# First two row blocks turned unscaled by the identity, 1/rms applied when v is read out and to the turned blocks afterwards

## The chip, the cores and the metric

The kernel runs on one core of a Trainium2 chip. The metric is device time in microseconds for one execution. Before the change three runs gave 1469.04, 1468.01 and 1468.40 us, a median of 1468.4 us. One more execution was profiled: 1468.83 us, of which 1467.0 us lie between the first and the last instruction of the core.

The engines named below are PE (matrix multiplication; PEld is its weight load), ACT (activations and copies), DVE (element-wise work), POOL, and SP, which here only issues transfers (DMAs). Each engine works through its own instructions in the order in which the program left them.

## The reference

One step of a layer with a recurrent branch and an attention branch. The part that the change touches is its start: the rows are RMS-normalised, turned and multiplied by the columns of `w_in` for v (1024 of them) and for the forget logits (16).

```
def rms_norm(x, g):
    y = xf * lax.rsqrt(jnp.mean(xf * xf, axis=-1, keepdims=True) + EPS)
    return (y * g).astype(x.dtype)

xn = rms_norm(x, g_pre)
z = xn @ w_in
xa, ga, q, k, v, gb, fl, ma, mb = jnp.split(z, ...)
logf = jax.nn.log_sigmoid(fl + b_f)
```

`x` has 1024 prompt rows and 64 sample rows of 1024 channels. v and logf are outputs of their own, and all later projections read the same normalised rows.

## The kernel before

**Tiles.** Rows go in blocks of 128 (blocks 0 to 7 are the prompt, block 8 the sample). PE contracts over channels, so every block is turned: eight 128x128 pieces, one for each channel group k. A turned block is kept as a high and a low part, `xh` (ACT copies it from PSUM with rounding) and `xl` (DVE subtracts). Weights are split in the same way: for each k a load `wv_raw` of 128x1024 (`load_wv`, two of the eight go to halves of `w_raw`) is copied to `wvh` by ACT and gives `wvl` on DVE (`split_wv`). The 16 forget columns come by a load of their own, `wf_raw`, 128 x 8 x 16 values in runs of 64 bytes, and stand behind the v columns in `wvh` and `wvl`.

**v of blocks 0 and 1.** `rows(b, ks)` multiplies block b by the weights of the groups ks: three passes (high by high, low by high, high by low) into three PSUM accumulators of 346, 346 and 348 columns, the last with the forget columns. A block needs all eight k, so the accumulators of both blocks stay open while the weights land, and PE alternates between the blocks. `evac_v` copies a finished accumulator out (`v_sb`) and sends it to memory.

**Turning.** For blocks 0 and 1 the inverse rms comes first (`rstd_diag`: a square with a sum on ACT, some small DVE steps with one square root on ACT between them), is put on a diagonal `dg`, and `turn_diag` multiplies x by this diagonal, so the turned values arrive scaled. Only `g_pre`, as a column `gT` per channel group, is left for ACT and DVE to apply (`x_hi`, `x_lo`). Blocks 2 to 8 are normalised first (`norm_x`: square, inverse rms, `scale_x` on DVE into the one buffer `xn`) and turned by the identity (`turn_x`, tile `tp`).

**What sets the order.** PE's order is written by hand for the whole program. For the opening, down to `norm_x(2)`, ACT's and DVE's orders are by hand too (`opening`); SP's and the later ACT and DVE work is ordered by a scheduler when the program is built. Dependences on PSUM are kept per bank: ACT and DVE take turns in reading one bank.

**Start of the clock.** 36 multiplications of the identity (`wake`, L440) run on PE before data are there, with the turning of `g_pre` (`g_p`, L439) among them.

**After the opening.** A loop goes over blocks 2 to 8: three accumulators each, with the next blocks turned at given places (`turn_at`). In it block 3 is turned after the first third of block 2, block 4 after block 2, block 5 after the first third of block 3, and so on. Then come sums of the turned blocks (`ra`, `rb`, `rc`), the column panels (`panel_steps`, `quad`), attention and the output stages. PE's order there is by hand as well.

Of the kernel before, what the change touches and what calls it, by code (L numbers as in the profile page):

```python
# [7 lines left out]
F32 = mybir.dt.float32  # L8
# [58 lines left out]
def hybrid_step(tc, a, o):  # L67
# [11 lines left out]
    def f(ap):  # L79
        return ap.bitcast(F32)  # L80

    def copy_act(out, in_, scale=1.0):
        return act.activation(out=out, in_=in_, func=AF.Copy, scale=scale)  # L83
# [42 lines left out]
    def tiny(n, name, w=1, tag=None):  # L126
        return small.tile([P, w], F32, name=name, tag=tag or name)[:n, :]
# [65 lines left out]
    def run(steps):  # L193
        for _ in steps:
            pass
# [188 lines left out]

    turned = {}

    def rstd_diag(b):
        x, junk = x_in[b], p1x.tile([P, D], F32, name="xn", tag="xn", bufs=1)  # L390
        r = tiny(P, "r_r")
        if b == 0:
            c, c_ = slice(0, D // 2), slice(D // 2, D)
            ss, rest = tiny(P, "ss"), tiny(P, "ss_")
            act.activation(out=junk[:, c], in_=x[:, c], func=AF.Square, accum_out=ss)
            dve.tensor_tensor_reduce(out=junk[:, c_], in0=x[:, c_], in1=x[:, c_], scale=1.0 / D, scalar=EPS,
                                     op0=ALU.mult, op1=ALU.add, accum_out=rest)
            rstd_of(ss, r, 1.0 / D, rest=rest)
        else:
            ss = tiny(P, "ss")  # L400
            act.activation(out=junk[:, :], in_=x[:, :], func=AF.Square, accum_out=ss)
            yield
            rstd_of(ss, r, 1.0 / D)
        dg = p1x.tile([P, P], F32, name="dg", tag="dg", bufs=2)
        dve.tensor_scalar(out=dg[:, :], in0=ident[:, :], scalar1=r, scalar2=None, op0=ALU.mult)
        turned[b] = dg
        yield

    def turn_diag(b):
        x, dg = x_in[b], turned[b]  # L410
        turned[b] = [p1t.tile([P, 4, P], F32, name="tp", tag="tp") for _ in range(2)]
        for k in range(KT):
            pe.matmul(turned[b][k // 4][:, k % 4, :], x[:, k * P:(k + 1) * P], dg[:, :], start=True, stop=True)

    def x_hi(b, ks):
        for k in ks:
            copy_act(xs[k][0][:, b * P:(b + 1) * P], turned[b][k // 4][:, k % 4, :], scale=gT[:, k:k + 1])

    def x_lo(b, ks):
        for k in ks:  # L420
            h, l = (t[:, b * P:(b + 1) * P] for t in xs[k])
            dve.scalar_tensor_tensor(out=l, in0=turned[b][k // 4][:, k % 4, :], scalar=gT[:, k:k + 1], in1=f(h),
                                     op0=ALU.mult, op1=ALU.subtract)

    g8 = p1.tile([KT, P], F32, name="g8")
    gT = p1.tile([P, KT], F32, name="gT")
    load_x(0)
# [4 lines left out]
    load_wv(1)  # L432
    for k in range(2, KT):
        load_wv(k)
    wake = p1t.tile([P, 512], F32, name="wake", tag="tp")
    g_p = mm.tile([P, 512], F32, name="g_p", tag="acc")
    for i in range(WAKE):
        if i == WAKE - 8:
            pe.transpose(g_p[:, :KT], g8[:, :], ident[:KT, :KT])  # L439
        pe.transpose(wake[:, :P], ident[:, :], ident[:, :])  # L440

    def weights(k, c):
# [1 line left out]
        return wvh[:, k, c0:c0 + w], wvl[:, k, c0:c0 + w]  # L444


    pair = [[p1v.tile([P, 512], F32, name="vacc", tag="vacc") for _ in VCH]]
    pair.append([p1v.tile([P, 512], F32, name="vacc", tag="vacc"),
                 mm.tile([P, 512], F32, name="acc", tag="acc"), mm.tile([P, 512], F32, name="acc", tag="acc")])

    def rows(b, ks):
        for k in ks:
            xh, xl = (t[:, b * P:(b + 1) * P] for t in xs[k])
            for p in (0, 2, 1):
                for c, (_, w) in enumerate(VCH):
                    wh, wl = weights(k, c)
                    pe.matmul(pair[b][c][:, :w], xl if p == 2 else xh, wl if p == 1 else wh,  # L457
                              start=(k == 0 and p == 0), stop=(k == KT - 1 and p == 1))

    opening = tc.manual_schedule(engines={act.engine, dve.engine})  # L460
    opening.__enter__()
    run(rstd_diag(0))
    dve.tensor_copy(gT[:, :], g_p[:, :KT])
    turn_diag(0)
    second = rstd_diag(1)
    split_wv(0)
    next(second)
    x_hi(0, [0])
    x_lo(0, [0])
    copy_act(wvh[:, :, D:], wf_raw[:, :, :])  # L470
    sub(dve, wvl[:, :, D:], wf_raw[:, :, :], f(wvh[:, :, D:]))
    x_hi(0, [1])
    x_lo(0, [1])
    rows(0, [0])
    run(second)
    split_wv(1)
    rows(0, [1])
    turn_diag(1)
    for ks in (range(2, 4), range(4, KT)):
        x_hi(0, ks)  # L480
        x_lo(0, ks)
    x_hi(1, (0, 1))
    x_lo(1, (0, 1))
    split_wv(2)
    rows(1, (0, 1))
    x_hi(1, range(2, KT))
    x_lo(1, range(2, KT))
    sp.dma_start(g_pre[:, :], a["g_pre"].partition_broadcast(P))
    load_x(2)
# [13 lines left out]
    def evac_v(b, c, acc):  # L503
        _, n, t0 = x_src[b]
        v_out = o["v_prompt"][t0:t0 + n, :] if b < NBLK else o["v_sample"]
        c0, w = VCH[c]
        wv = min(w, D - c0)
        v_sb = p1.tile([P, VCH[-1][1]], F32, name="v_sb", tag="v_sb", bufs=3)
        copy_act(v_sb[:n, :wv], acc[:n, :wv])
        if b == NBLK:  # L510
            lo = p1.tile([DEC, VCH[-1][1]], F32, name="v_lo", tag="v_lo", bufs=1)
            copy_act(lo[:, :w], acc[DEC:, :w])
            dve.tensor_tensor(out=v_sb[:n, :wv], in0=acc[:n, :wv], in1=lo[:, :wv], op=ALU.add)
        act.dma_start(v_out[:, c0:c0 + wv], v_sb[:n, :wv])
        if wv < w:
            dve.tensor_tensor(out=fl[:n, b, :], in0=acc[:n, wv:w], in1=bf[:n, :], op=ALU.add)
            if b == NBLK:
                dve.tensor_tensor(out=fl[:n, b, :], in0=fl[:n, b, :], in1=lo[:, wv:w], op=ALU.add)

    for k in range(2, 6):  # L520
        split_wv(k + 1)
        rows(0, [k])
        rows(1, [k])
    split_wv(7)
    norm_x(2)
    opening.__exit__(None, None, None)
    rows(0, (6, 7))
    for c in range(3):
        evac_v(0, c, pair[0][c])
    rows(1, [6])  # L530
# [1 line left out]
    rows(1, [7])  # L532
    for c in range(3):
        evac_v(1, c, pair[1][c])

# [1602 lines left out]
```

## Time and profile before

| | |
|---|---|
| median of three runs | 1468.4 us (1468.01 to 1469.04) |
| profiled execution | 1468.83 us |
| its span on the core | 1467.0 us |
| granted PE clock, mean | 0.996 |
| DVE busy | 59% |
| ACT busy | 49% |
| v rows of block 0 finished on PE | 36.37 us |
| block 2 turned on PE | 37.80 us |
| first v rows of block 2 on PE | 40.10 us |

Times in the last three rows, and in every timeline row, are counted from the first instruction. A timeline row has start, duration, engine, source line, operation, output and inputs, shape and count, and in brackets the idle time of the engine before it with what ended it. A window row has the stretch, its length, busy time of engines with instruction counts, the granted PE clock, the busy share of the transfer engines, and GB/s. "x16" at L413 are eight multiplications of which each shows as two records.

### The profile page before, as it was taken

How to read it: one execution, taken by the hardware profiler on the slowest of the kernel's cores; microseconds unless marked ns; L12 is line 12 of the kernel's file. 1: busy time of each engine (PE TensorE's matmuls, PEld its weight loads, DVE VectorE, ACT ScalarE, POOL GpSimd, SP SyncE). 2: the span in 40 equal slices, each digit the busy share in tenths (PEclk: the TensorE clock that was granted, in tenths of full speed). 3: DMA queues.
4: the chain of work that ended last, by engine and by line, in shares of the span. 5: the costliest groups of instructions: out<-in, count | busy, mean ns of one | idle time of the engine just before them, and what ended most of it. 6: DMA issues, size and time to landing. Idle time of an engine off the chain costs nothing.

```text
span 1467.0 us, 26370 instructions
## 1 busy us (share of the span) xinstructions
PE 1442.0 (98%) x10117; PEld 1419.7 (97%) x10117; DVE 871.6 (59%) x1571; ACT 718.0 (49%) x1388; POOL 276.3 (19%) x363
## 2 busy tenths in 40 slices
PE   9999999999999999999999999999999999999997
PEld 8998999999999999999999999999999999999997
DVE  5564756665525666666556557798755454347644
ACT  4423444443215566656555557877543333334633
POOL 0012314323113333333223210000023000000001
PEclk9999999999999999999999999999999999999999
DMA  5367456655276565646556242121386534214111
GB/s 205 108 130 97 122 167 185 186 164 136 75 215 160 119 147 135 142 115 158 92 125 157 51 101 49 50 57 33 130 269 214 194 130 141 85 37 164 47 48 44
DMA packets 140793, 182.85 MB, mean 125 GB/s; under 512 B 22788, under 2 KB 111404, under 8 KB 140668
## 3 DMA queue, kind: packets, MB, share of 16 engines
q1 hardware_dynamic: 122684, 154.90, 40.3%
q10 hardware_dynamic: 17680, 25.64, 5.0%
q8 instruction: 80, 1.31, 0.4%
q0 software_dynamic: 304, 0.62, 0.1%
q14 instruction: 45, 0.37, 0.1%
HBM read 122.65 MB, written 58.46 MB: 123 GB/s over the span
## 4 chain that ended last, share of the span: by engine, by line
PE 91%; DVE 3%; ACT 3%; DMA 2%; issue 1%; ACTq 0%; SPq 0%; DVEq 0%
PE quad L786 17%; PE acc L163 16%; PE acc L164 16%; PE acc L165 16%; PE tp L1132 4%; PE pv L1160 3%; PE pv L1162 3%; PE s L1110 2%; PE s L1111 2%; PE vacc L163 1%; PE vacc L164 1%; PE vacc L165 1%; PE vacc L457 1%; DMA out_v_prompt<-v_sb 1%; DMA wv_raw<-in_w_in 1%; DMA q<-d_q 1%
## 5 line engine op out<-in xcount | busy, mean ns | idle before, releaser
L163 PE MATMUL acc<-xh,wh 128*128 128x364 f32 (+1 forms) x768 | 253.6, 330 | 3.1 <-ACT st L83 3.1
L164 PE MATMUL acc<-xl,wh 128*128 128x364 f32 (+1 forms) x768 | 252.5, 329 | 0.0
L165 PE MATMUL acc<-xh,wl 128*128 128x364 f32 (+1 forms) x768 | 252.4, 329 | 0.0
L163 PEld LDWEIGHTS acc<-xh,wh 128*128 128x128 f32 x768 | 145.2, 189 | 4.1 <-ACT st L83 3.4
L164 PEld LDWEIGHTS acc<-xl,wh 128*128 128x128 f32 x768 | 145.1, 189 | 0.5
L165 PEld LDWEIGHTS acc<-xh,wl 128*128 128x128 f32 x768 | 144.7, 188 | 0.0
L86 DVE TENSOR_TENSOR wl<-w_raw,wh 128x1024 fp32r<-128x1024 f32 (+1 forms) x66 | 76.9, 1168 | 64.1 <-ACT wh L83 56.2
L1090 DVE CUSTOM_DVE_ANT_0 s<-s,mask 128x1024 f32<-128x1024 f32 (+7 forms) x128 | 95.5, 767 | 26.1 <-PE s L1111 25.8
L83 ACT ACTIVATE wh<-w_raw 128x1024 fp32r<-128x1024 f32 (+1 forms) x66 | 64.3, 976 | 76.6 <-PE acc L164 35.1
L1095 POOL TENSOR_SCALAR pb<-pb,sm 128x896 f32<-128x896 f32 (+1 forms) x64 | 61.5, 961 | 203.8 <-DVE sm L1094 186.6
L86 DVE TENSOR_TENSOR tl<-tp,th 128x512 fp32r<-128x512 f32 x96 | 65.8, 689 | 36.6 <-ACT th L83 36.6
L786 PE MATMUL quad<-xh,wh 128*128 128x272 f32 x384 | 80.8, 292 | 0.0
L786 PE MATMUL quad<-xl,wh 128*128 128x272 f32 x384 | 79.5, 289 | 0.0
L786 PE MATMUL quad<-xh,wl 128*128 128x272 f32 x384 | 79.5, 288 | 0.0
L1092 ACT ACTIVATE pb<-s,nm 128x896 f32<-128x896 f32 (+1 forms) x64 | 61.1, 954 | 33.3 <-DVE nm L1090 26.8
L83 ACT ACTIVATE th<-tp 128x512 fp32r<-128x512 f32 x96 | 56.9, 596 | 40.1 <-PE tp L1132 36.1
L163 PE MATMUL acc<-wqh,hth 128*128 128x256 f32 x256 | 72.9, 285 | 0.0
L164 PE MATMUL acc<-wql,hth 128*128 128x256 f32 x256 | 72.2, 282 | 0.0
L165 PE MATMUL acc<-wqh,htl 128*128 128x256 f32 x256 | 72.2, 282 | 0.0
L165 PE MATMUL acc<-wqh,mxl 128*128 128x256 f32 x256 | 71.7, 280 | 0.0
L163 PE MATMUL acc<-wqh,mxh 128*128 128x256 f32 x256 | 71.7, 280 | 0.0
L164 PE MATMUL acc<-wql,mxh 128*128 128x256 f32 x256 | 71.6, 280 | 0.0
(550 smaller groups left out, 4202.4 us busy)
## 6 DMA issues: line engine op xcount, KB each, us to landing
w_raw<-in_w_in SPq DMA_DIRECT2D x60, 256.0 KB
q<-d_q SPq DMA_DIRECT2D x48, 256.0 KB
k<-d_k SPq DMA_DIRECT2D x48, 256.0 KB
w_raw<-in_w_branch SPq DMA_DIRECT2D x32, 256.0 KB
w_raw<-in_w_in SPq DMA_DIRECT2D x56, 128.0 KB
wraw<-in_w_in SPq DMA_DIRECT2D x20, 256.0 KB
d_k<-oh ACTq DMA_DIRECT2D x16, 272.0 KB
d_k<-kl SPq DMA_DIRECT2D x16, 272.0 KB
```

The lines of the kernel that those rows point to most:

```text
L83: return act.activation(out=out, in_=in_, func=AF.Copy, scale=scale)
L86: return eng.tensor_tensor(out=out, in0=in0, in1=in1, op=ALU.subtract)
L163: pe.matmul(out, ah, bh, start=start, stop=False)
L164: pe.matmul(out, ah, bl, start=False, stop=False)
L165: pe.matmul(out, al, bh, start=False, stop=stop)
L786: pe.matmul(acc[:, c, :CW], l[:, k, :], r[:, k, c * CW:(c + 1) * CW], start=(first and k == 0 and p == 0), stop=(k == 3 and p == 2), skip_ ...
L1090: at = book("D", now[0] + HOP_PE, per(D_MAX, n), lambda: dve.tensor_tensor_reduce(out=s[:, :n], in0=s[:, :n], in1=m, scale=-1.0, scalar=-N ...
L1092: free = book("A", at, per(A_EXP, n), lambda: act.activation(out=pr[:, :n], in_=s[:, :n], func=AF.Exp, scale=-1.0, bias=nm, accum_out=sm))
L1095: return free, book("G", at, per(G_NORM, n), lambda: pool.tensor_scalar(out=pr[:, :n], in0=pr[:, :n], scalar1=sm, scalar2=1.0, op0=ALU.mul ...
L1132: pe.transpose(tp[:, o0 + i * P:o0 + (i + 1) * P], pr[par][:, kb * P:(kb + 1) * P], ident[:, :])
L1160: pe.matmul(pv[:, :256], v, tl[:, c], start=(g == 0 and j == 0), stop=False)
L1162: tc.declare_no_dep(pe.matmul(pv[:, :256], v, th[:, c], start=False, stop=(g == q2 and j == 1)).ins, high.ins, reason="ordered through the ...
```

## The change

The inverse rms leaves the opening. Blocks 0 and 1 are turned as they land, by the identity (`turn_raw`), into four PSUM banks which hold both blocks side by side, two k to a bank; for k from 2 on one ACT and one DVE instruction (`x_hl`) make the high and the low part of both blocks at once. v is summed from unscaled rows, and `evac_v` multiplies by the inverse rms of the row while it reads the accumulator out (`both`, a column for each block). The turned blocks themselves are put right later: `spread_both` lays the 256 inverse rms values along a row for all partitions (a diagonal by a matrix of ones on PE, copied to `r_row` by ACT), and `scale_turned`, called in four steps from the loop over blocks 2 to 4, adds high and low, multiplies by `r_row` and splits again.

The first weight load is cut into two halves of 512 columns. The forget columns are loaded after the weights of k = 3 and multiplied for k below 4 in a sweep of their own. There are 12 `wake` instructions instead of 36. SP's order in the opening is by hand too.

```diff
-WAKE = 36
+WAKE = 12
...
-    def rstd_diag(b):
...
-    def turn_diag(b):
...
+    def turn_raw(b):
+        x = x_in[b]
+        for k in range(KT):
+            if b == 0 and k % 2 == 0:
+                pl, tag = turned[k // 2]
+                turned[k // 2] = pl.tile([P, 512], F32, name=f"{tag}_x", tag=tag)
+            pe.transpose(raw_part(k, b), x[:, k * P:(k + 1) * P], ident[:, :])
...
+    def x_hl(k, b, n=1):
+        h, l = (t[:, b * P:(b + n) * P] for t in xs[k])
+        copy_act(h, raw_part(k, b, n), scale=gT[:, k:k + 1])
+        dve.scalar_tensor_tensor(out=l, in0=raw_part(k, b, n), scalar=gT[:, k:k + 1], in1=f(h),
+                                 op0=ALU.mult, op1=ALU.subtract)
...
+    opening = tc.manual_schedule(engines={act.engine, dve.engine, sp.engine})
...
     load_x(0)
     act.dma_start(g8[:, :], a["g_pre"].rearrange("(k p) -> k p", p=P))
-    load_wv(0)
+    for c in first_cols:
+        sp.dma_start(first_raw[:, c], w_in[:P, C_V + c.start:C_V + c.stop])
     load_x(1)
+    for k in range(1, 4):
+        load_wv(k)
     sp.dma_start(wf_raw[:, :, :], w_in[:, C_FL:C_FL + NH].rearrange("(k p) n -> p k n", p=P))
...
+    turn_raw(0)
+    x_hl(0, 0)
+    for c in first_cols:
+        copy_act(wvh[:, 0, c], first_raw[:, c])
+        sub(dve, wvl[:, 0, c], first_raw[:, c], f(wvh[:, 0, c]))
+    rows(0, [0], (0, 1))
+    turn_raw(1)
+    x_hl(1, 0)
+    x_hl(0, 1)
+    rows(1, [0], (0, 1))
+    x_hl(1, 1)
+    split_wv(1)
+    load_wv(4)
+    load_wv(5)
+    rows(0, [1], (0, 1))
+    rows(1, [1], (0, 1))
+    for k in (2, 3):
+        x_hl(k, 0, 2)
+        split_wv(k)
+        rows(0, [k], (0, 1))
+        rows(1, [k], (0, 1))
+    load_wv(6)
     copy_act(wvh[:, :, D:], wf_raw[:, :, :])
     sub(dve, wvl[:, :, D:], wf_raw[:, :, :], f(wvh[:, :, D:]))
+    rows(0, range(4), (2,))
+    rows(1, range(4), (2,))
+    for k in range(4, KT):
+        x_hl(k, 0, 2)
+    for b in range(2):
+        act.activation(out=xn[:, :], in_=x_in[b][:, :], func=AF.Square, accum_out=ss2[:, b:b + 1])
+    load_x(2)
+    load_wv(7)
...
-        copy_act(v_sb[:n, :wv], acc[:n, :wv])
+        copy_act(v_sb[:n, :wv], acc[:n, :wv], both[:, b:b + 1] if b < 2 else 1.0)
...
+    def spread_both():
+        for b in range(2):
+            dve.tensor_scalar(out=dg[:, :], in0=ident[:, :], scalar1=both[:, b:b + 1], scalar2=None, op0=ALU.mult)
+            pe.matmul(r_p[:, :P], ones[:, :], dg[:, :], start=True, stop=True)
+            copy_act(r_row[:, b * P:(b + 1) * P], r_p[:, :P])
+    def scale_turned():
+        for g in range(2):
+            for j in range(0, 4, 2):
+                h, l = XH[g][:, j:j + 2, :n], XL[g][:, j:j + 2, :n]
+                tc.keep_in_program_order(dve.tensor_tensor(out=t, in0=f(h), in1=f(l), op=ALU.add))
+                for i in range(2):
+                    dve.tensor_tensor(out=t[:, i, :], in0=t[:, i, :], in1=r_row[:, :], op=ALU.mult)
+                copy_act(h, t)
+                sub(dve, l, t, f(h))
+                yield
...
-    for k in range(2, 6):
-        split_wv(k + 1)
+    for k in range(4, KT):
+        split_wv(k)
         rows(0, [k])
-        rows(1, [k])
-    split_wv(7)
+        if k == 5:
+            rstd_both()
+        if k < 6:
+            rows(1, [k])
+    spread_both()
     norm_x(2)
     opening.__exit__(None, None, None)
-    rows(0, (6, 7))
...
             evac_v(b, c, acc)
+            if c == 1:
+                for _ in range(2 if b == 2 else 1):
+                    next(scaling, None)
```

Where the rows of the orders move, three places matter. The first is SP's queue from its first transfer on (`x_in` are the blocks of x, `w_raw` takes the weights of k = 3 and 4). Before:

```order
L325 DMA x_in<-in_x_prompt 128x1024
L335 DMA wv_raw<-in_w_in 128x1024
L325 DMA x_in<-in_x_prompt 128x1024
L431 DMA wf_raw<-in_w_in 128x8x16
L335 DMA wv_raw<-in_w_in 128x1024 x2
L335 DMA w_raw<-in_w_in 128x1024 x2
```

and with the change:

```order
L325 DMA x_in<-in_x_prompt 128x1024
L422 DMA wv_raw<-in_w_in 128x512 x2
L325 DMA x_in<-in_x_prompt 128x1024
L335 DMA wv_raw<-in_w_in 128x1024 x2
L335 DMA w_raw<-in_w_in 128x1024
L426 DMA wf_raw<-in_w_in 128x8x16
L335 DMA w_raw<-in_w_in 128x1024
L335 DMA wv_raw<-in_w_in 128x1024 x2
L325 DMA x_in<-in_x_prompt 128x1024
```

The forget columns have moved behind three weight loads.

The second is ACT from the last weight splits to the turned block 2 (L348 is the square of `norm_x`, L138 its root, `xh<-tp` the turned block 2). Before:

```order
L83 ACTIVATE wvh<-wv_raw 128x1024 x3
L348 ACTIVATE xn,ss<-x_in 128x1024
L138 ACTIVATE r_y<-r_v 128x1
L83 ACTIVATE v_sb<-vacc 128x346 x2
L514 DMA out_v_prompt<-v_sb 128x346 x2
L83 ACTIVATE v_sb<-vacc 128x332
L514 DMA out_v_prompt<-v_sb 128x332
L83 ACTIVATE xh_108<-tp 128x4x128
```

and with the change:

```order
L83 ACTIVATE wvh<-wv_raw 128x1024 x2
L83 ACTIVATE v_sb<-vacc,both 128x346 x2
L83 ACTIVATE r_row<-r_p 128x128 x2
L348 ACTIVATE xn,ss<-x_in 128x1024
L510 DMA out_v_prompt<-v_sb 128x346
L138 ACTIVATE r_y<-r_v 128x1
L510 DMA out_v_prompt<-v_sb 128x346
L83 ACTIVATE v_sb<-acc,both 128x332
L510 DMA out_v_prompt<-v_sb 128x332
L83 ACTIVATE xh_108<-tp 128x4x128
```

The square of block 2 has moved behind the read-out of two accumulators of block 0 and behind the two copies of `r_row`; PE makes `r_p` directly after the last rows of block 0.

The third is ACT in the loop, from block 2's second accumulator to the turned block 4. Before:

```order
L83 ACTIVATE v_sb<-vacc 128x346
L514 DMA out_v_prompt<-v_sb 128x346
L83 ACTIVATE v_sb<-vacc 128x332
L514 DMA out_v_prompt<-v_sb 128x332
L83 ACTIVATE xh_108<-tp 128x4x128
```

and with the change:

```order
L83 ACTIVATE v_sb<-vacc 128x346
L510 DMA out_v_prompt<-v_sb 128x346
L83 ACTIVATE xh_108<-wv_raw 128x2x256
L83 ACTIVATE v_sb<-vacc 128x332
L510 DMA out_v_prompt<-v_sb 128x332
L83 ACTIVATE xh_108<-wv_raw 128x2x256
L83 ACTIVATE xh_108<-tp 128x4x128
```

Two steps of `scale_turned` have come in, the second directly ahead of the turned block 4.

More of the change, by code (lines that the diff above doesn't have):

```diff
@@ L383, in turn_x @@
                 pool.tensor_copy(xsl[:, 4 * g:4 * g + 4, DEC:], f(l))
-    turned = {}
-    def rstd_diag(b):
[L390 to L407, printed above, removed]
@@ L409, in turn_diag @@
-    def turn_diag(b):
-        x, dg = x_in[b], turned[b]
-        turned[b] = [p1t.tile([P, 4, P], F32, name="tp", tag="tp") for _ in range(2)]
-        for k in range(KT):
[L413 to L423, printed above, removed]
+    both = p1.tile([P, 2], F32, name="both")
@@ L428, in hybrid_step @@
     act.dma_start(g8[:, :], a["g_pre"].rearrange("(k p) -> k p", p=P))
-    load_wv(0)
+    first_raw = p1x.tile([P, D], F32, name="wv_raw", tag="wv_raw", bufs=3)
+    first_cols = (slice(0, D // 2), slice(D // 2, D))
+    for c in first_cols:
+        sp.dma_start(first_raw[:, c], w_in[:P, C_V + c.start:C_V + c.stop])
     load_x(1)
+    for k in range(1, 4):
+        load_wv(k)
     sp.dma_start(wf_raw[:, :, :], w_in[:, C_FL:C_FL + NH].rearrange("(k p) n -> p k n", p=P))
-    load_wv(1)
-    for k in range(2, KT):
-        load_wv(k)
@@ L435, in hybrid_step @@
-    wake = p1t.tile([P, 512], F32, name="wake", tag="tp")
-    g_p = mm.tile([P, 512], F32, name="g_p", tag="acc")
     for i in range(WAKE):
-        if i == WAKE - 8:
+        if i == WAKE - 2:
             pe.transpose(g_p[:, :KT], g8[:, :], ident[:KT, :KT])
@@ L444, in weights, with rows @@
         return wvh[:, k, c0:c0 + w], wvl[:, k, c0:c0 + w]
[L447 to L451, printed above, removed]
+    def rows(b, ks, cs=(0, 1, 2)):
         for k in ks:
@@ L454, in rows @@
             for p in (0, 2, 1):
-                for c, (_, w) in enumerate(VCH):
+                for c in cs:
+                    w = VCH[c][1]
                     wh, wl = weights(k, c)
@@ L458, in rows @@
                               start=(k == 0 and p == 0), stop=(k == KT - 1 and p == 1))
-    opening = tc.manual_schedule(engines={act.engine, dve.engine})
-    opening.__enter__()
-    run(rstd_diag(0))
     dve.tensor_copy(gT[:, :], g_p[:, :KT])
[L464 to L469, printed above, removed]
+    turn_raw(0)
+    pair = [[p1v.tile([P, 512], F32, name="vacc", tag="vacc") for _ in range(2)] for _ in range(2)]
+    x_hl(0, 0)
[19 more added lines that the diff above has]
+    load_wv(6)
     copy_act(wvh[:, :, D:], wf_raw[:, :, :])
     sub(dve, wvl[:, :, D:], wf_raw[:, :, :], f(wvh[:, :, D:]))
[L472 to L487, printed above, removed]
+    for p in pair:
+        p.append(mm.tile([P, 512], F32, name="acc", tag="acc"))
+    rows(0, range(4), (2,))
+    rows(1, range(4), (2,))
+    for k in range(4, KT):
+        x_hl(k, 0, 2)
+    ss2 = tiny(P, "ss2", 2)
+    for b in range(2):
+        xn = p1x.tile([P, D], F32, name="xn", tag="xn", bufs=1)
+        act.activation(out=xn[:, :], in_=x_in[b][:, :], func=AF.Square, accum_out=ss2[:, b:b + 1])
+    load_x(2)
+    load_wv(7)
     sp.dma_start(g_pre[:, :], a["g_pre"].partition_broadcast(P))
-    load_x(2)
     load_x(3)
@@ L534, in hybrid_step @@
         evac_v(1, c, pair[1][c])
+    scaling = scale_turned()
     def blk(g, h):
```

20 lines of the change are left out of this document (19 added, 1 removed).

## The prediction

> **What bounds the kernel now.** I read the page first, then the timeline of PE and the windows of the opening, then ACT's and DVE's timelines at the places where PE stood.
>
> ```profile
> PE 1442.0 (98%) x10117; PEld 1419.7 (97%) x10117; DVE 871.6 (59%) x1571; ACT 718.0 (49%) x1388; POOL 276.3 (19%) x363
> ```
>
> PE is never without work for long, so only its waits and its half-rate stretches are there to be won. The edit touches the opening and the loop over blocks 2 to 4. Here is PE there, and then its granted clock (the three window rows that follow "..." are of PE alone, the last two of all engines):
>
> ```profile
> 1.60 6.06 PE L440 MATMUL wake<-ident 128*128 128x128 f32 x28 [1.60 <-POOL ident L111]
> 8.68 1.95 PE L413 MATMUL tp<-dg,x_in 128*128 128x128 f32 x16
> 10.38 0.56 PE L457 MATMUL vacc<-wvh,xh 128*128 128x346 f32 x2
> 11.98 0.43 PE L457 MATMUL vacc<-wvh,xh 128*128 128x348 f32 x1 [1.04 <-ACT wvh L83]
> 14.35 1.24 PE L457 MATMUL vacc<-wvh,xh 128*128 128x346 f32 x3 [0.99 <-ACT wvh L83]
> 17.12 2.18 PE L413 MATMUL tp<-dg,x_in 128*128 128x128 f32 x16
> 36.37 0.32 PE L457 MATMUL vacc<-wvh,xh 128*128 128x346 f32 x1
> 37.80 1.03 PE L377 MATMUL tp<-ident,xn 128*128 128x128 f32 x8
> 38.59 0.41 PE L457 MATMUL vacc<-wvh,xh 128*128 128x346 f32 x1
> 40.10 0.32 PE L163 MATMUL vacc<-wvh,xh 128*128 128x346 f32 x1
> 44.95 1.29 PE L377 MATMUL tp<-ident,xn 128*128 128x128 f32 x8 [0.74 <-DVE xn L361]
> 59.22 1.29 PE L377 MATMUL tp<-ident,xn 128*128 128x128 f32 x8 [0.56 <-ACT v_sb L83]
> ...
> 1.60:7.42 5.82, 5.82 (x28) 1.00 0.92 278
> 7.75:8.68 0.93, 0.93 (x10) 1.00 0.53 157
> 14.35:17.12 2.77, 2.77 (x10) 0.50 0.96 380
> ...
> 14.00:15.00 1.00, 0.65 (x2) 0.65 (x3) 0.83 (x2) 1.00 (x5) 0.00 (x0) 0.59 1.05 411
> 17.00:18.00 1.00, 1.00 (x8) 1.00 (x7) 0.11 (x1) 0.00 (x0) 0.00 (x0) 0.70 0.64 240
> ```
>
> The first v rows start at 10.38. PE then stands twice, about 1 us each time, and the clock falls to half from about 14.2 (0.59 in that microsecond) to 17.6 (0.70), 3.4 us. From 17.6 PE does not wait until the turning of block 3 (0.74 ahead of 44.95): block 0 is done at 36.37 and block 2's rows start at 40.10. Nine multiplications take 2.77 us at half rate (0.30 each) and 1.43 at full (36.37 to 37.80, 0.159 each); a turning by the identity takes 0.79 (37.80 to 38.59). The clock is low at the very start too, whatever its column says: 28 `wake` instructions take 5.82 us (0.208 each), the eight after them 0.93 (0.116).
>
> What PE waits for is data, then ACT and DVE behind them:
>
> ```profile
> 4.27 0.63 ACT L395 ACTIVATE xn<-x_in 128x512 f32<-128x512 f32 x1 [1.33 <-DMA x_in<-in_x_prompt]
> 6.54 1.06 ACT L83 ACTIVATE wvh<-wv_raw 128x1024 fp32r<-128x1024 f32 x1 [1.06 <-DMA wv_raw<-in_w_in]
> 7.93 1.06 ACT L401 ACTIVATE xn<-x_in 128x1024 f32<-128x1024 f32 x1 [0.33 <-DMA x_in<-in_x_prompt]
> 11.62 0.31 ACT L83 ACTIVATE wvh<-wf_raw 128x128 fp32r<-128x128 f32 x1 [1.48 <-DMA wf_raw<-in_w_in]
> 13.24 1.06 ACT L83 ACTIVATE wvh<-wv_raw 128x1024 fp32r<-128x1024 f32 x1 [0.37 <-DMA wv_raw<-in_w_in]
> 10.17 0.35 DVE L422 SCALAR_TENSOR_TENSOR xl<-tp,gT,xh 128x128 fp32r<-128x128 f32 x1 [1.01 <-ACT xh L83]
> 14.33 1.23 DVE L86 TENSOR_TENSOR wvl<-wv_raw,wvh 128x1024 fp32r<-128x1024 f32 x1 [0.17 <-ACT wvh L83]
> 9.77 0.37 ACT L83 ACTIVATE xh<-tp,gT 128x128 fp32r<-128x128 f32 x1 [0.69 <-PE tp L413]
> ```
>
> All five ACT rows ended a wait for a transfer, so they give the landings: x at 4.27, weights of k = 0 at 6.54, second x at 7.93 (1.4 us for 512 KB), forget columns at 11.62 (3.7 us for 64 KB, in 64-byte runs), weights of k = 1 at 13.24, two microseconds behind what 1.4 us each would give.
>
> **The change part by part.** *Landings.* With the forget columns behind k = 3, each load takes about 1.4 us: k = 1 at 9.4, k = 2 at 10.8, k = 3 at 12.2, forget columns at 12.2 + 3.7 = 15.9. Bounds for these: 13.3 if only bytes counted, 19.6 if the 64-byte runs take twice as long beside other loads. I take 15.9, the row itself.
>
> *First rows.* The 12 `wake` instructions end at about 4.3, when x lands; eight turnings at 0.208 end at 6.0. The halved weights land at about 5.5 and 6.7; ACT takes 0.63 (the 128x512 row) and DVE about 0.7 for a half, so the last low half is ready at 8.0, and the six multiplications end at 8.9 (0.30 each, clock still low). Block 1 is turned by 10.5. Its parts share one bank with block 0's k = 1, so ACT and DVE alternate, 0.37 and 0.35, three times: 9.5 to 11.9. Then ACT splits k = 1 (to 12.5), DVE follows (to 13.7). PE stands in between, and from 13.8 has data: a k costs ACT about 1.5 us and DVE 1.7, against 12 x 0.159 = 1.9 on PE.
>
> *From 13.8 on.* PE has 2 + 6 multiplications of k = 1, 24 of k = 2 and 3, 24 of the forget sweep: 56 x 0.159 = 8.9, to 22.7. Meanwhile ACT, in its order, waits for the forget columns (15.9), splits them (0.3), makes four pairs of blocks in turn with DVE (from the 0.37 and 0.35 rows about 0.45 each for twice the width, 3.3 in all), squares two blocks and gets to the weights of k = 4 at 22.0, ready at 23.0. So the late forget columns cost nothing up to 15.5 and a microsecond each from there: 0.4 here, and 0.3 more behind DVE's part. Six more groups of nine (8.6 us) end block 0 at 32.0 instead of 36.37: **-4.4**. The saved PE work is in it: a turning of 1.70 us (8.68 to 10.38) becomes 0.79, twice.
>
> *Block 2's turning.* This is where the gain goes.
>
> ```profile
> 27.18 1.05 ACT L348 ACTIVATE xn<-x_in 128x1024 f32<-128x1024 f32 x1
> 28.63 0.20 ACT L138 ACTIVATE r_y<-r_v 128x1 f32<-128x1 f32 x1 [0.32 <-DVE r_v L135]
> 29.84 1.42 DVE L361 SCALAR_TENSOR_TENSOR xn<-x_in,r_r,g_pre 128x512 f32<-128x512 f32 x2
> 36.25 0.81 ACT L83 ACTIVATE v_sb<-vacc 128x346 f32<-128x346 f32 x2 [7.41 <-PE vacc L457]
> 44.05 1.42 DVE L361 SCALAR_TENSOR_TENSOR xn<-x_in,r_r,g_pre 128x512 f32<-128x512 f32 x2
> ```
>
> Before, block 2 was normalised at 27.18 to 31.3, far ahead of its turning at 37.80. Now its square stands on ACT behind two read-outs of block 0 and two copies of `r_row`, and both wait for PE to end block 0: 32.0, read-outs to 33.0 (0.81 for two), `r_row` to 33.5 (two of some 0.37). From the square to the scaling takes 29.84 - 27.18 = 2.66 us, from there to the turning 44.95 - 44.05 = 0.90: 33.4 + 3.6 = 37.0. PE has only `r_p` (0.4) and one group of nine (1.43) for that time, is done at 33.8 and stands **3.1 us**. Queued behind the turning on PE are the last nine of block 1, and all of block 2 behind these. So -4.4 + 0.4 + 3.1 = **-0.9** is left at block 2's turning (36.9 to 37.0, instead of 37.80).
>
> *What the wait does to the clock.* Earlier, two waits of 1 us each in about 3.4 us halved it for 3.4 us. A wait of 3.1 us should do so again: the turning and the last nine of block 1 then end at 40.5 rather than 39.4. But the turning of block 3 (44.95) waited 0.74 us for a chain on ACT and DVE, which takes up part of it; block 3 is turned 0.65 us earlier than before if the clock holds, at the same time if not.
>
> *The Trainium skill*, TensorE: Matmul & The Clock Gate, Part 1, has the clock drop after an idle window of about 3.4 us that runs freely; the 3.4 us at half rate here agree. Its Part 4 says that transposes do not count as PE activity for the clock. The `wake` instructions are transposes, and 28 of them took the pace from 0.208 to 0.116, so this trace does not bear it out; by that rule the clock here would come up only after 14 us (the third rival).
>
> *Scaling in the loop.*
>
> ```profile
> 54.39 0.17 DVE L516 TENSOR_TENSOR fl<-vacc,bf 128x16 f32<-128x16 f32 x1 [3.63 <-ACT v_sb L83]
> 54.78 1.09 ACT L83 ACTIVATE xh<-tp 128x512 fp32r<-128x512 f32 x2 [0.42 <-PE tp L377]
> 56.93 0.15 DVE L135 TENSOR_SCALAR r_v<-ss 128x1 f32<-128x1 f32 x1 [0.23 <-ACT xn L348]
> 68.67 0.17 DVE L516 TENSOR_TENSOR fl<-vacc,bf 128x16 f32<-128x16 f32 x1 [3.64 <-ACT v_sb L83]
> L86 DVE TENSOR_TENSOR wl<-w_raw,wh 128x512 fp32r<-128x512 f32 x2 | 1.4, 683 | 0.0
> L86 DVE TENSOR_TENSOR xl<-tp,xh 128x256 fp32r<-128x256 f32 x2 | 0.7, 416 | 0.0
> L83 ACT ACTIVATE wh<-s 128x512 fp32r<-128x512 f32 x3 | 1.9, 626 | 0.8 <-ACT oh L83 0.4 <-ACT kl L83 0.4
> ```
>
> One step is on DVE an addition (0.68), two products (some 0.4 each) and a subtraction (0.68), 2.1 us, and 0.63 on ACT. DVE's idle time of 3.6 us ahead of 68.67 covers the single steps of blocks 3 and 4; were it gone, they would cost 2 us each. Block 2 has two steps, 4.2 us against 3.63 idle, and the second copy on ACT stands right ahead of the turned block 4, at 54.78. It delays that by 0.6 and, with DVE's second subtraction in front, the mean square of block 5 (56.93) by 0.85. Block 5's turning (59.22) already ends a wait for this chain: **+0.85**. The scale on the read-outs and on the forget logits rides in instructions that are there anyway. The inverse rms of both blocks (about 1.2 us of small steps) lies between two weight splits, beside PE's 2.9 us of k = 5.
>
> *Sum.* At block 3's turning -0.65 to 0, at block 5's +0.2 to +0.85, and nothing after that: the orders of the later stages stand as before and start from PE's progress. I take +0.5: the profiled 1468.83 becomes 1469.3, and the median of 1468.4, which stands 0.4 below the profiled execution, becomes **1468.9 us**. A measurement of this kernel can hardly tell less than 0.2%, 2.9 us, from no change; this is no change.
>
> **The rivals.** *Faster: PE never stands at block 2's turning.* If the square of block 2 ran in ACT's idle time before 32 us, the early rows would be kept: -4.4 + 0.4 = -4.0, +0.85 in the loop, 1465.3. For it speaks ACT's 7.41 us of idle time ahead of 36.25; against it the order itself, in which the square follows `r_row`, and that follows PE. 0.10.
>
> *Slower: the forget columns hold ACT up.* Everything that ACT does for k = 4 to 7 is queued behind their split. Each microsecond after 15.5 is a microsecond of PE, so slower than before from about 15.5, and slower by 2.9 us from a landing at 18.3. At the upper bound of 19.6 it is +0.5 + 3.7: 1472.6. For it: 3.7 us for 64 KB, now in the middle of a stream of weights; against it: the same 3.7 us were taken beside loads then too. 0.14.
>
> *The clock stays low longer*, since fewer `wake` instructions leave PE idle at 6 to 7.4 and 12 to 13.8. One more stretch of 3.4 us at half rate behind 13.8 costs 1.7: 1470.6. For it: two waits of 1 us in 3.4 were enough for it at 14.2; against it: PE is busy nearly all of 7.4 to 11. 0.14.
>
> **How the numbers follow.** My forecast has 0.62. Its own range is 1468.0 to 1470.0. The first rival is faster (0.10), the second mostly slower (0.12 of 0.14), the third mostly no change, with 0.03 slower where it meets a late landing; of the forecast 0.02 is left for each side, for work later on that meets other transfers. Faster 0.12, no change 0.71, slower 0.17. The range goes from 1465.9 to 1472.0 and leaves out the first rival and half of the second.
>
> **What would show it.** Right: first v rows near 6 us, PE standing about 3 us ahead of block 2's turning with ACT or DVE as releaser, that turning within 1 us of 37.8, half clock around 38 to 41, and a longer wait ahead of block 5's turning (1.4 us where there was 0.56). Wrong: no such wait, or ACT waiting for `wf_raw` beyond 17 us, or a difference of more than 1 us that arises after block 5's turning.

## The result, and the profile after

The changed kernel takes 1473.2 us (median of 6 runs, 1469.3 to 1477.7) against 1468.2 for the kernel before, measured beside it (1465.4 to 1469.6): a ratio of 1.0041, 95% interval 1.0026 to 1.0056. It is slower by about 0.4%. The profiled execution took 1474.2 us with a span of 1472.2 (before 1468.83 and 1467.0). 1468.9 was forecast, with a range up to 1472.0.

| | before | after |
|---|---|---|
| median of the runs, us | 1468.2 | 1473.2 |
| PE busy in the profiled execution, us | 1442.0 | 1445.8 |
| multiplications and turnings on PE | 10117 | 10081 |
| mean granted clock | 0.996 | 0.995 |

PE does less work (36 instructions fewer) and is busy 3.8 us longer. The page of the changed kernel:

```profile
PE 1445.8 (98%) x10081; PEld 1421.1 (97%) x10081; DVE 874.7 (59%) x1574; ACT 721.3 (49%) x1388; POOL 274.2 (19%) x363
```

The opening first. This is PE's timeline of the changed kernel: start, duration, line, what it does, and in brackets the idle time ahead with what ended it.

```profile
4.61 1.06 PE L400 MATMUL acc_x<-ident,x_in 128*128 128x128 f32 x4
7.25 1.34 PE L444 MATMUL vacc<-wvh,xh 128*128 128x346 f32 x2 [0.73 <-ACT wvh L83]
...
32.25 0.61 PE L531 MATMUL r_p<-dg,ones 128*128 128x128 f32 x4
36.81 1.46 PE L377 MATMUL tp<-ident,xn 128*128 128x128 f32 x8 [2.53 <-DVE xn L361]
40.67 0.49 PE L163 MATMUL vacc<-wvh,xh 128*128 128x346 f32 x1
44.75 1.29 PE L377 MATMUL tp<-ident,xn 128*128 128x128 f32 x8
53.50 1.03 PE L377 MATMUL tp<-ident,xn 128*128 128x128 f32 x8
59.90 1.29 PE L377 MATMUL tp<-ident,xn 128*128 128x128 f32 x8 [1.44 <-DVE xn L361]
```

Block 0 is done at 32.25 (36.37 before), and then PE stands 2.53 us ahead of block 2's turning. What ACT does meanwhile, from its timeline of the same kernel:

```profile
6.57 1.32 ACT L83 ACTIVATE wvh<-wv_raw 128x512 fp32r<-128x512 f32 x2 [0.93 <-DMA wv_raw<-in_w_in]
16.81 0.31 ACT L83 ACTIVATE wvh<-wf_raw 128x128 fp32r<-128x128 f32 x1 [0.60 <-DMA wf_raw<-in_w_in]
32.13 0.99 ACT L83 ACTIVATE v_sb<-vacc,both 128x346 f32<-128x346 f32 x2 [3.67 <-PE vacc L444]
33.32 1.08 ACT L348 ACTIVATE xn<-x_in 128x1024 f32<-128x1024 f32 x1
54.94 0.63 ACT L83 ACTIVATE xh<-wv_raw 128x512 fp32r<-128x512 f32 x1 [0.79 <-DVE wv_raw L542]
```

The square of block 2 runs at 33.32 and not at 27.18. In the last row ACT waits 0.79 us for DVE's part of a `scale_turned` step, ahead of the turned block 4. Behind PE's wait of 2.53 us the clock is half, as the window of PE alone shows (length, busy time, instructions, granted clock, share of the DMA engines, GB/s):

```profile
38.00:41.00 3.00, 3.00 (x13) 0.50 0.51 175
```

So at block 5's turning (59.90, before 59.22) the changed kernel is 0.68 us behind, which the prediction had between 0.2 and 0.85. All the rest of the loss arises later. The same places on PE, first in the kernel before, then in the changed one:

```profile
144.14 0.67 PE L163 MATMUL acc<-xh,wh 128*128 128x364 f32 x1 [3.06 <-ACT st L83]
163.69 0.52 PE L786 MATMUL quad<-t3h,wh 128*128 128x272 f32 x2 [0.87 <-DVE u__1642 L872]
739.09 0.50 PE L1110 MATMUL s<-k,q 128*128 128x512 f32 x1 [1.72 <-ACT pb L1092]
988.55 0.43 PE L163 MATMUL gacc<-uh,g_h 128*128 128x364 f32 x1 [2.37 <-ACT r_e L1595]
1061.71 0.44 PE L165 MATMUL acc<-yah,wl 128*128 128x364 f32 x1 [1.53 <-DVE wl L86]
1459.22 0.28 PE L165 MATMUL acc<-wqh,htl 128*128 128x256 f32 x1
```

```profile
141.99 0.43 PE L163 MATMUL acc<-xh,wh 128*128 128x364 f32 x1 [0.20 <-ACT st L83]
160.11 0.52 PE L819 MATMUL quad<-t3h,wh 128*128 128x272 f32 x2 [0.87 <-DVE u__1626 L905]
271.04 0.39 PE L830 MATMUL tpk<-ident,ko 128*32 128x128 f32 x2 [1.02 <-ACT kst L83]
445.64 0.55 PE L1165 MATMUL tp<-ident,pm 128*128 128x128 f32 x3 [0.92 <-POOL pm L1128]
739.50 0.50 PE L1143 MATMUL s<-k,q 128*128 128x512 f32 x1 [2.50 <-ACT pb L1125]
990.23 0.67 PE L163 MATMUL gacc<-uh,g_h 128*128 128x364 f32 x1 [2.37 <-ACT r_e L1628]
1064.59 0.44 PE L165 MATMUL acc<-yah,wl 128*128 128x364 f32 x1 [1.40 <-DVE wl L86]
1464.48 0.28 PE L165 MATMUL acc<-wqh,htl 128*128 128x256 f32 x1
```

Each difference is after less before. It is -3.6 at 160 us: the kernel before had waited 3.06 us, with half clock behind. It is +0.4 at 739, +1.7 at 989, +2.9 at 1062 and +5.3 at the last multiplication. Two kinds of loss show in PE's windows. The kernel before, then the changed one:

```profile
741.00:744.00 3.00, 2.97 (x22) 1.00 0.91 210
991.00:993.00 2.00, 2.00 (x14) 1.00 0.05 15
...
1290.00:1330.00 40.00, 40.00 (x343) 1.00 0.16 50
1250.00:1450.00 200.00, 200.00 (x1709) 1.00 0.21 71
```

```profile
741.00:744.00 3.00, 3.00 (x14) 0.50 0.78 191
991.00:993.00 2.00, 2.00 (x8) 0.50 0.24 58
...
1290.00:1330.00 40.00, 40.00 (x337) 1.00 0.14 42
1250.00:1450.00 200.00, 200.00 (x1683) 1.00 0.22 73
```

Behind 741 and 991 the clock is half in the changed kernel alone, though the wait ahead of the second place is 2.37 us in both. From 1250 to 1450 neither kernel waits and both have the full clock, yet PE starts 26 multiplications fewer in the same 200 us. At 200/1709 = 0.117 us apiece that is 3.0 us, and no row of the profile names a cause.

### The profile page after: what moved, and what is told of

Read it like the earlier page. It is cut to its first block, busy times and chain, and to the rows that moved or that the text cites. A ratio compares the mean times of both kernels' runs of the same rounds, so it can differ in the third digit from the quotient of the medians.

```text
span 1472.2 us, 26307 instructions
## 1 busy us (share of the span) xinstructions
PE 1445.8 (98%) x10081; PEld 1421.1 (97%) x10081; DVE 874.7 (59%) x1574; ACT 721.3 (49%) x1388; POOL 274.2 (19%) x363
## 4 chain that ended last, share of the span: by engine, by line
PE 89%; DVE 4%; ACT 3%; DMA 3%; issue 1%; POOL 0%; ACTq 0%; DVEq 0%; SPq 0%; POOLq 0%
PE quad L819 16%; PE acc L163 16%; PE acc L164 16%; PE acc L165 16%; PE tp L1165 4%; PE pv L1193 3%; PE pv L1195 3%; PE s L1143 2%; PE s L1144 2%; PE vacc L163 1%; PE vacc L164 1%; PE vacc L165 1%; PE vacc L444 1%; DMA q<-d_q 1%; PE tp L1962 1%
## 5 line engine op out<-in xcount | busy, mean ns | idle before, releaser
L86 DVE TENSOR_TENSOR wl<-w_raw,wh 128x1024 fp32r<-128x1024 f32 (+1 forms) x66 | 76.8, 1166 | 63.9 <-ACT wh L83 63.4
```

Of the source, the lines that this page charges most:

```text
L86: return eng.tensor_tensor(out=out, in0=in0, in1=in1, op=ALU.subtract)
```

## The experiments

The ratios below are to the kernel before, run beside each on the same chip, with their 95% intervals. The count is PE's instructions between 1250 and 1450 us in each profile.

| kernel | median, us | ratio | count |
|---|---|---|---|
| before again | 1466.9 | 1.0001 [0.9988, 1.0014] | 1709 |
| change again | 1475.7 | 1.0051 [1.0038, 1.0065] | 1683 |
| change, first weights in one transfer | 1471.8 | 1.0034 [1.0021, 1.0047] | 1682 |
| before, first weights in two transfers | 1466.4 | 0.9987 [0.9974, 1.0001] | 1709 |
| change, small tiles elsewhere | 1469.05 | 1.0009 [0.9997, 1.0020] | 1710 |
| before, three idle small tiles more | 1471.3 | 1.0026 [1.0015, 1.0036] | 1682 |
| before, 15 wake instructions | 1467.2 | 0.9999 [0.9988, 1.0011] | 1709 |
| change, block 2 normalised first | 1469.6 | 1.0013 [0.9999, 1.0026] | 1682 |
| the same, small tiles elsewhere | 1467.6 | 0.9993 [0.9982, 1.0003] | 1708 |
| block 2 first, operands 64 bytes apart | 1460.4 | 0.9946 [0.9930, 0.9962] | 1755 |
| before, operands 64 bytes apart | 1465.0 | 0.9978 [0.9963, 0.9994] | 1739 |
| before, operands 32 bytes apart | 1468.3 | 1.0002 [0.9987, 1.0016] | 1694 |

**Does it repeat, and is it the number of transfers?** Loading the first weights in halves adds one transfer. From there on every transfer of the program shares its completion counter with others than before. This was the first theory (A); that the later places are chance (B) and that the loss is in the opening (C) were its rivals. Four kernels: the change and the kernel before once more, and both with that one transfer taken the other way.

> The changed kernel once more, for a second profile. Its first profile stood +0.7 us behind the kernel before from 60 to 130 us, 2.4 to 3.6 ahead from 141 to 430, and fell back to +5.2 by 1460. Theory A (the change leaves something behind for the whole kernel, such as one transfer more, which moves later waits): the ratio stays at 1.003 to 1.005 and the waits of PE stand at the same places as in the first profile (2.5 us near 740, 1.0 near 270). Theory B (which microseconds stand where is chance, from the phase of the clock and of transfers): the waits and the half-rate stretches lie elsewhere; the ratio is 1.000 to 1.002.

> The kernel before once more, for a second profile and as the measure of chance. All theories: ratio 1.000 within 0.0015. Theory A: its wait of 3.06 us ahead of 143 and the pace of the last 200 us are as in its first profile. Theory B: they differ by several microseconds between two profiles of one kernel.

The edit of the third, and the reverse of it in the fourth:

```diff
-    for c in first_cols:
-        sp.dma_start(first_raw[:, c], w_in[:P, C_V + c.start:C_V + c.stop])
+    sp.dma_start(first_raw[:, :], w_in[:P, C_V:C_V + D])
```

> The changed kernel with the first weights loaded in one transfer (still split in halves on ACT and DVE), so that the number of transfers is that of the kernel before. The first v rows come about 1 us later, since the weights land at 6.5 rather than 5.5 and 6.7, of which block 2's turning shows less than 0.3, as PE waits there anyway. Theory A: each later transfer waits for the same earlier ones as in the kernel before, and the ratio falls from 1.004 to 1.000 to 1.001 (1468.3 to 1470). Theory B, and a theory C by which the loss is in the opening: 1.003 to 1.005 as the change itself.

> The kernel before with the first weights loaded in two transfers and nothing else changed: one transfer more, so that every later transfer shares its completion counter with others than before. The opening moves by less than 0.3 us. Theory A: 1.003 to 1.004, slower by 4 to 6 us, all of it behind 60 us. Theories B and C: 0.999 to 1.001.

The loss repeats: 1.0051. Theory A falls: the kernel before with one transfer more is not slower (0.9987), and the change with one transfer less keeps most of its loss (1.0034). C falls too: at block 5's turning the change was 0.68 us behind in the first pair of profiles, and in the second (59.8 against 60.3) it was ahead. B expected 1.000 to 1.002 for the change and missed, so chance is not the whole of the loss, but it is right for some of the places. The wait of 3.06 us near 141 came back in the second profile of the kernel before, but it was 0.53 in another kernel with the same orders and the same number of transfers (three idle tiles more). The change with one transfer has 1.63 us of it. From each profile one row of PE: the kernel before again, then with three idle tiles, then the change with one transfer.

```profile
145.52 0.67 PE L163 MATMUL acc<-xh,wh 128*128 128x364 f32 x1 [3.40 <-ACT st L83]
```

```profile
141.92 0.43 PE L166 MATMUL acc<-xh,wh 128*128 128x364 f32 x1 [0.53 <-ACT st L83]
```

```profile
142.89 0.43 PE L163 MATMUL acc<-xh,wh 128*128 128x364 f32 x1 [1.63 <-ACT st L83]
```

What did not vary is the last 200 us: 1709 in both profiles of the kernel before, 1683 in both of the change. The loss there belongs to the change.

**What slows PE by 1.5% without a wait.** Two things differ for instructions whose order, shape and operands are the same. First, the change has nine kinds of tiles in the pool `small` where there were six. That pool opens early and closes last; the built program gives each of its tiles 32 bytes and two buffers, so everything allocated on that side after it lies 3 x 2 x 32 = 192 bytes higher: `wqh` at 60896 instead of 60704, `hth` at 112096 instead of 111904, while `mxh`, from the other side, stays at 143328 (theory D). Second, PE's stream is shorter by 36 instructions with their weight loads, so that everything after them stands in another place of the stream (theory E).

```diff
-    ss2 = tiny(P, "ss2", 2)
+    ss2 = p1.tile([P, 2], F32, name="ss2")[:, :]
+    tiny(P, "ss_")
...
-    rstd_of(ss2, both[:, :], 1.0 / D, tmp=[tiny(P, f"b_{c}", 2) for c in "vyt"])
+    rstd_of(ss2, both[:, :], 1.0 / D, tmp=[p1.tile([P, 2], F32, name=f"b_{c}")[:, :] for c in "vyt"])
```

> The changed kernel with the four new small tiles (ss2, b_v, b_y, b_t) taken from the pool p1, which closes after the v stage, instead of the pool `small`, which lasts to the end. Every tile allocated after `small` then lies where it does in the kernel before, 192 bytes lower than in the change; instructions, their order and their waits are those of the change. Theory D (the addresses set PE's pace): the 128x256 multiplications of 1250 to 1460 us go back from a steady 0.120 us to about 0.1175, worth 3 us, and the waits of 0.6 to 1.0 near 270 and 0.4 to 1.5 near 437 to 445 may go too: 1469.5 to 1471.5, ratio 1.001 to 1.002. Theory E (the place of PE's instructions, 71 fewer in its stream, sets the pace): 1.004 to 1.005 as the change, pace 0.120.

The reverse, in the kernel before:

```diff
+    for i in range(3):
+        small.tile([P, 1], F32, name=f"pad{i}", tag=f"pad{i}")
```

> The kernel before with three unused one-number tiles in the pool `small`, which shift every later tile by 192 bytes, to where they lie in the change; instructions, order and waits are those of the kernel before. Theory D: pace 0.120 from 1250 to 1460 us, +3 us, waits near 270 and 440 if they hang on addresses: 1471 to 1473, ratio 1.002 to 1.003. Theory E: 1.000, pace 0.1175.

And the place in the stream alone, with WAKE = 15 instead of 36 in the kernel before:

> The kernel before with 15 wake instructions instead of 36, so that PE's later instructions stand 42 places earlier in its stream; addresses as before. Theory E: the pace of the last 200 us changes from 0.1175 (to 0.120 if the place decides as it does in the change). Theory D: it stays at 0.1175. In the opening the clock is half when block 0 is turned at 8.7 us, which costs 1 to 2 us there: 1468 to 1470.5.

PE's windows of the three, in this order:

```profile
1250.00:1450.00 200.00, 200.00 (x1710) 1.00 0.21 71
```

```profile
1250.00:1450.00 200.00, 200.00 (x1682) 1.00 0.21 71
```

```profile
1250.00:1450.00 200.00, 200.00 (x1709) 1.00 0.21 71
```

The count follows the addresses: 1710 in the change with the old addresses, 1682 in the kernel before with the new ones, 1709 with another place in the stream. The first two profiles and nine of the table have one placing or the other, and all agree: 1708 to 1710 with the old addresses, 1682 or 1683 with the new ones. The ratios go with it. Theory D stands, and E falls. Half clock that comes by chance does not explain the ratio either: of the executions with a mean granted clock of 0.995, seven of the kernel before took 1467.2 to 1470.0 us, five with the three idle tiles 1470.4 to 1473.0. Three tiles of one number each, which nothing reads or writes, make the kernel before slower by 0.26%; giving the change its old addresses back takes it from 1.0041 and 1.0051 to 1.0009. One part of the expectation failed: the waits near 270 and 445 us are no matter of addresses. They were there in the change with the old addresses (1.04 us at 270.9) and not in the kernel before with the new ones. With 15 wake instructions the expected half clock at 8.7 us did not come either: the clock was full from 5.2 to 12.1 us and half from there to 18.9, and the median is not longer than before.

**The wait ahead of block 2's turning.** The order that the prediction named (the square of block 2 behind the spreading of the inverse rms, and that behind PE) can be turned round by exchanging two lines:

```diff
-    spread_both()
     norm_x(2)
+    spread_both()
```

> The changed kernel with block 2 normalised ahead of the spreading of both inverse rms over a row. Its square then starts near 26 us instead of 33.3, and PE's wait of 2.5 us ahead of block 2's turning is gone: that turning at 34.3 instead of 36.8, no half clock at 38 to 41, and 1.5 to 2.5 us are gained if nothing later takes them up; the waits ahead of the turnings of block 3 (none in the change) and block 5 (1.4) are likely to grow by as much, since the scaling stands ahead of them on DVE: ratio 1.002 to 1.005. Theories D and E: the pace of the last 200 us is 0.120 as in the change.

PE's timeline of that kernel, and its window where the clock was half in the change:

```profile
32.80 0.68 PE L531 MATMUL r_p<-dg,ones 128*128 128x128 f32 x4 [0.43 <-DVE dg L529]
34.76 1.03 PE L377 MATMUL tp<-ident,xn 128*128 128x128 f32 x8
42.14 1.29 PE L377 MATMUL tp<-ident,xn 128*128 128x128 f32 x8 [1.11 <-DVE xn L361]
50.89 1.03 PE L377 MATMUL tp<-ident,xn 128*128 128x128 f32 x8
57.12 1.29 PE L377 MATMUL tp<-ident,xn 128*128 128x128 f32 x8 [1.27 <-DVE xn L361]
```

```profile
37.80:41.00 3.20, 3.20 (x21) 1.00 0.43 149
```

The wait is gone, the clock holds (the wait is not all that half clock hangs on: the last section has a profile with the wait and the full clock), and block 5 is turned at 57.12 instead of 59.90, 2.8 us earlier than in the change and 2.1 earlier than before the change. A wait of 1.1 us ahead of block 3's turning takes a part, as expected; the one ahead of block 5 did not grow (1.27 us, 1.44 in the change), and the ratio of 1.0013 is better than the expected 1.002 to 1.005. It stands lower than the change's by 0.3 to 0.4%, more than the 2.8 us of the profile, within the intervals. The pace at the end is the change's (1682).

> Both remedies in the changed kernel: block 2 normalised ahead of the spreading, and the four small tiles in p1, so that all later tiles lie where they do in the kernel before. Theory D: the pace from 1250 to 1460 us is 0.1175 again, and the 3.2 us that the profile of the norm-first kernel lost there are back: 1465 to 1467, ratio 0.998 to 0.9995. If the two do not add up, 1.001.

Both remedies together give 0.9993, which can't be told from the kernel before. That is 0.0020 below block 2 first alone, as much as the 3.0 us of the trace, and the count is 1708.

**Which addresses are good.** For each 128x256 multiplication between 1225 and 1440 us I took the time from its start to the next one's start out of the trace, and grouped these by where the built program puts the first byte of the operand that moves (`wqh`, `wql`, and `wph`, `wpl` of the last projection) and of the one that is loaded as weights (`mxh`, `hth`, their low halves, and `mxs` for the sample rows), modulo 128. Some ten times of 200 ns and more in each profile hold a wait and are left out.

| kernel | moving, loaded | count | mean ns |
|---|---|---|---|
| before | 32, 32 | 733 | 119.3 |
| before | 96, 96 | 192 | 119.9 |
| before | 32, 96 | 575 | 116.3 |
| before | 96, 32 | 200 | 115.2 |
| change | 96, 96 | 1668 | 119.7 |

With 192 more bytes on one side, all pairs of the change start at the same place. About 770 multiplications of the kernel before that took some 116 ns take 119.7: 2.8 us of the 3.0. If the distance decides, pads can make it 64 bytes for all of them but those of the last projection:

```diff
     mix = [tuple(mxpool.tile([P, T], F32R, name=f"mx{i}{of}") for i in "hl") for of in range(KT)]
+    mxpool.tile([P, 16], F32, name="pad_m")
...
+    hpool.tile([P, 16], F32, name="pad_h")
     wq = sb("wq", bufs=3)
     tpool = sb("tpool")
+    tpool.tile([P, 16], F32, name="pad_t")
```

In the norm-first kernel the two outer pads do it; the kernel before needs all three. With 32 bytes, the outer two have 8 numbers instead of 16, and the middle one is left out.

> The norm-first kernel with two pads of 64 bytes (after the mix tiles, ahead of the tiles hth and htl), so that in the last 250 us the operand that moves and the one that is loaded as weights always start 64 bytes apart modulo 128; instructions, order and waits as in the norm-first kernel. In the two profiles of the kernel before and of the change, multiplications whose two operands start at the same place modulo 128 took 119.3 to 119.9 ns apiece, and those 64 bytes apart 115.2 to 116.3. By this rule about 1660 multiplications gain 4 ns: pace 0.1155 to 0.1165, 6 to 7 us less than the norm-first kernel: 1462.5 to 1464, ratio 0.995 to 0.997. If only the place of the weights' tiles decides, not the distance, 0.120 and 1.001.

> The kernel before with three pads of 64 bytes, so that the operands of the last 250 us start 64 bytes apart modulo 128 throughout, where 915 of 1690 started at the same place; nothing else changed. By the rule of the distance 915 times 4 ns: 3.5 us less, 1464 to 1465, ratio 0.997 to 0.998. If the distance does not decide: 1.000.

> The kernel before with two pads of 32 bytes, so that the operands of the last 250 us start 32 bytes apart modulo 64 throughout. If what counts is whether both start at the same place modulo 128, this is as good as 64 bytes apart: 1464 to 1465, pace 0.1155 to 0.1165. If it is the distance of 64 that helps, 0.118 to 0.120 and 1.000 to 1.003.

PE's windows of the three, in this order:

```profile
1250.00:1450.00 200.00, 200.00 (x1755) 1.00 0.21 71
```

```profile
1250.00:1450.00 200.00, 200.00 (x1739) 1.00 0.22 71
```

```profile
1250.00:1450.00 200.00, 200.00 (x1694) 1.00 0.20 68
```

By the same grouping, 1566 pairs of the first kernel at 96 and 32 took 114.2 ns, 1558 of the second 115.2. Those 32 bytes apart took 119.0 (1166 of them, 32 and 64) and 117.2 (383, 96 and 64). The pads do not change the last projection: its two operands still start at the same place in all three kernels (119.1 to 119.4 ns).

The order of the three distances is not the same everywhere. Take the first of the four weight quarters and the other three apart, for the output weights and for the gate. The same place took 119.6 to 119.9 ns in all four groups (48 multiplications of the sample rows aside, 116.9), 64 bytes 113.3 to 117.8, and 32 bytes 116.7 to 119.7, which is no gain in the largest group. So the same place is worst, 64 bytes apart is best on the whole, and 32 saves little. What makes the rest of the difference was not found.

The first kernel, norm-first with two pads, takes 1460.4 us, 0.5% less than the kernel before and about 1% less than the change. That is better than the 1462.5 to 1464 expected, since a pair gained 5.5 ns and not 4. It is the best version here.

## Why the prediction was wrong

**The landings: near.** The forget columns were waited for until 16.8 instead of 15.9, and ACT's first split ran at 6.57, with the first v rows at 7.25 instead of near 6. Neither cost anything that is seen later. (The lower bound of 13.3 for the forget columns does not follow from the rows: 64 KB at 1.4 us for 512 KB behind 12.2 give 12.4. Nothing hangs on it.)

**-4.4 for the early rows, +0.4 for `r_p`: right in size, in part by luck.** Block 0 ends at 32.25, forecast 32.0. But the sum had PE stand before 13.8 and then lose 0.7 us to ACT and DVE behind the late forget columns; by its rule of a microsecond each from 15.5, the landing at 16.8 would have cost 1.3. In the trace PE worked all the while from 7.25 on, at first at half rate, and hardly waited up to 24.4:

```profile
8.39 0.78 PE L444 MATMUL vacc<-wvh,xl 128*128 128x346 f32 x2
14.84 0.48 PE L444 MATMUL vacc<-wvh,xh 128*128 128x346 f32 x2
...
13.30:24.40 11.10, 11.02 (x67) 1.00 0.49 157
```

A multiplication took 0.29 us near 8.4 (the next row starts at 8.97) and 0.16 near 14.8. So the clock was low about as long as the forecast assumed; the further stretch of half rate behind 13.8 of the third rival did not come.

**The wait of 3.1 us ahead of block 2's turning: right**, with 2.53 us, the turning at 36.8 (36.9 to 37.0 forecast) and the releaser in DVE's and ACT's chain. That this order is the cause of the wait is shown: with two lines exchanged the wait goes. **Half clock from 38 to 41: right here**, but the wait does not bring it each time (last section), and block 3's turning at 44.75 lies within the forecast of 0.65 to 0 ahead.

**+0.2 to +0.85 at block 5's turning: right**, +0.68, with the wait at 1.44 us as named.

**"and nothing after that: the orders of the later stages stand as before and start from PE's progress": wrong.** This is the step that failed, and with it its premise that at PE "only its waits and its half-rate stretches are there to be won". The prediction took PE's pace as fixed and put the later stages at nothing. The orders do stand as before, but the same order is not the same time. Three more kinds of tiles in a pool that lasts to the end move the later tiles by 192 bytes, and PE does its last 200 us 3.0 us slower, without a wait and at the full clock. The prediction costed every instruction and every transfer that the change adds, and no byte. The condition it set for being wrong ("a difference of more than 1 us that arises after block 5's turning") is what happened; none of its rivals had it.

**The range: too narrow on its upper side.** The kernel before ran between 1464.1 and 1475.7 us across all comparisons. Of the +5.0 in the medians, the change with its old addresses keeps 1.3 (1.0009), near the forecast of +0.5. The addresses make 3.0 us in the trace and 3.8 by the reverse experiment (1.0026, 2.2 to 5.3); what is left is smaller than the intervals.

**Left open.** The waits of about 1 us near 270 and 445 us stood in both profiles of the change and in neither of the kernel before; with block 2 normalised first they were absent in one profile and back, in part shorter, in two others. They follow neither the addresses nor the number of transfers. What they hang on was not tried.

## What to carry to other kernels

Two kernels with the same orders can differ by where their tiles lie: put temporary tiles into a pool that closes with its stage, and after an edit compare the addresses of what PE reads later. Where PE is bound by its own pace, count its instructions in a window without waits; if the count differs at the same clock, look at the addresses. And before a difference of a few microseconds in one profile is explained, take a second profile of each kernel.

## What the runs showed of the hardware

The time of a 128x256 multiplication with its weight load depends on the distance modulo 128 between the two operands' first bytes: in the mean 119 to 120 ns at the same place, 117 to 119 at 32 bytes, 114 to 116 at 64. I had taken this pace as fixed. For the wider multiplications of the middle of the kernel no rule was worked out.

A wait does not always bring half clock. The same 2.37 us near 986 had it behind them in the first profile of the change and not in that of the kernel before. The wait ahead of block 2's turning had it in the change's two profiles. The change with one transfer had the same wait and the full clock behind it, and a mean granted clock of 0.999:

```profile
36.85 1.23 PE L377 MATMUL tp<-ident,xn 128*128 128x128 f32 x8 [2.54 <-DVE xn L361]
...
38.00:41.00 3.00, 3.00 (x21) 1.00 0.56 175
```

Where it came, it lasted 3.4 us, which cost some 1.7 us, or twice that (12.0 to 18.8 us in the kernel before with its operands 64 bytes apart), and where it comes differs between two profiles of one kernel. Much of the spread of one kernel's executions goes with it: beside the last four kernels, the kernel before took 1468.9 and 1472.4 us with a mean granted clock of 0.993, and 1464.8 and 1465.7 with 0.998.
